# A decoder layer on one core: rotating q and k from the product banks, inverse roots as logarithm, exponential and correction, and the sums of squares as two single-rate products

## The chip, the cores and the metric

One core of a Trainium2 chip runs the whole program. The metric is the device time of one execution in microseconds (us); lower is better. Three executions of the kernel before are given, and one further execution was recorded by the profiler.

## The reference, cut to what matters

One layer with 1024 channels, 2048 prompt columns and 8 sample columns. All arithmetic is float32.

```
h  = RMSNorm(x)*(1+scale1)+shift1          # scale, shift, g from silu(c) @ w_ada
[u | q | k | v | a_pool | a_attn] = h @ w_in
q = rope(rmsnorm_per_head(q) * q_norm_g)   # 12 heads of 64, 3 groups of 4 heads
k = rope(rmsnorm_per_head(k) * k_norm_g)
x += g1 * ( sig(a_pool)*(PoolMix(u) @ w_pool_br) + sig(a_attn)*(DilatedAttn(q,k,v) @ w_attn_br) ) @ w_out
h2 = RMSNorm(x)*(1+scale2)+shift2
x += g2 * relu(h2 @ w_up)^2 @ w_down
```

rmsnorm multiplies by 1/sqrt(mean of squares + 1e-6); rope maps the halves (a, b) of each head to (a cos - b sin, b cos + a sin).

## The kernel before

**Numbers.** A float32 product is made of three products of the rounded type F32R: each operand is split into a high part (a cast) and a low part (the difference), and `mm3` runs high x high, high x low, low x high. The weights are split by ScalarE (`wh`, L183) and GpSimd (`wh`, L184) as their loads arrive; activations are split where they are made. A plain float32 product also exists (`small`, L168), which the kernel uses for sums over channels.

**Stages, in the order of the trace.** Columns go in two halves: ci=0 has 1032 columns (pieces of 512, 256 and 264; the last holds the 8 samples), ci=1 has 1024 (two of 512). The opening (to about 81 us) makes the modulation and the first normed columns. qkv(0) follows (to about 295 us) with six PSUM banks for products; gates, sample attention and the pool branch come to about 745 us; then qkv(1) runs with two banks only, with the prompt's attention between its products (to about 1140 us); more attention and the merger to 1380 us; w_out, the second norm and the MLP to the end at 3060 us.

**One job of q or k** is one group g of four heads (2 x 128 channels: the heads' first halves in i=0, second halves in i=1), q or k, and one piece of columns: 18 jobs in qkv(0) (six of each size), 12 in qkv(1). For each, `dense` fills two banks `ps_qk` of 24 matmuls each. `qk_out` reads each bank twice on ScalarE: L390 copies it with the norm's gain to `ab`, L391 squares it to `qsq`. Then the generator `after_qk` runs: SyncE loads the cosines and sines `cs` (L404, 512 KB), GpSimd adds the two squares (L405) and makes two of the four products of the rotation (L409, L411), VectorE the other two (L410, L412) and the sum and the difference `ro` (L413, L414). At `yield HS_AT` it sleeps for 6500 ns of TensorE's planned time; then TensorE sums squares over each head's channels with the fp32 matmul `ps_hs` against the 0/1 matrix `hones` (L417, which is part of the constants `cp`), ScalarE takes the root (L419), VectorE the reciprocal (L420) and the two products with it (L422). ScalarE and GpSimd split the result into `ohl` (L444, L445), one buffer, which SyncE stores to `qst` or `kst` in HBM (L450 to L456).

**Order.** TensorE's program order is worked out by class `Order`: each matmul adds its planned nanoseconds to `now`, and a generator that yields a number is resumed when `now` has passed it. So the place of `ps_hs` among the dense products is fixed in the program. The other engines' orders are set by the Tile framework's scheduler from the same program, with a higher priority for what stands under `first()`. Each engine works through its own list in order, and an instruction that waits holds all behind it. SyncE issues all loads and stores from one list.

**The norms of x** go through `rms_finish`: a fp32 matmul with `ones` gives the sum of squares, then the same pair of root (L313, ScalarE) and reciprocal (L314, VectorE); ten times in all, two of them (`rs0`, `rs1`) in the opening.

## Time and profile before

| what | value |
|---|---|
| median of 3 runs | 3061.22 us (3057.11 to 3063.97) |
| the profiled execution's own time | 3062.32 us |
| its span, first to last instruction | 3060.5 us |
| TensorE busy | 2933.8 us (96%) |
| ScalarE, GpSimd, VectorE busy | 982.3, 966.2, 1590.5 us |
| mean granted TensorE clock | 0.980 |

TensorE is busy nearly all the time, so a change shows in the time where it shortens TensorE's own work, or where it makes TensorE wait more or less. The share is a mean over stages; the windows in the section of rows keep them apart. A granted clock of 1.00 is TensorE's upper level of 2.4 GHz and 0.50 the lower of 1.2 GHz; a window's value between them is a mean.

### The profile page before, as it was taken

The page shows a single profiled execution, that of the slowest core. Times are in us where ns is not written, and L with a number is a line of the kernel's source. Part 1 is how long each engine was busy: PE and PEld are TensorE (multiplying, and loading weights), DVE is VectorE, ACT ScalarE, POOL GpSimd, SP SyncE. Part 2 cuts the span into 40 slices and gives each one's busy share as a digit, 9 for nine tenths or more (in the row PEclk, how much of TensorE's full clock was granted, in tenths as well). Part 3 has the DMA queues.
Part 4 walks back from the last instruction along what each step waited for, and adds up shares of the span by engine and source line. Part 5 has one row for each costly group of instructions (what it writes and reads, how often), then busy time and mean ns, then how long its engine had stood idle before and what let it go on. Part 6 is the DMA issues. An engine that isn't in the chain of part 4 may idle for free.

```text
span 3060.5 us, 40917 instructions
## 1 busy us (share of the span) xinstructions
PE 2933.8 (96%) x16220; PEld 2510.3 (82%) x16220; DVE 1590.5 (52%) x2649; ACT 982.3 (32%) x1772; POOL 966.2 (32%) x510
## 2 busy tenths in 40 slices
PE   6899999999898799999999999999999999999999
PEld 3899788887787688878899999999877888888887
DVE  5556442541744534456865545555677554444444
ACT  5333342433554534433521221121235211111211
POOL 2665341433533312233532122122245312221221
PEclk7999999999999889999999999999999999999999
DMA  6544752335777779876321111111272211111111
GB/s 239 172 144 154 270 183 92 118 118 151 200 196 203 186 191 229 239 243 218 105 78 48 43 49 49 42 51 47 92 242 83 76 42 56 48 49 42 55 43 69
DMA packets 207599, 379.09 MB, mean 124 GB/s; under 512 B 47424, under 2 KB 103072, under 8 KB 206624
## 3 DMA queue, kind: packets, MB, share of 16 engines
q1 hardware_dynamic: 195888, 359.63, 38.6%
q10 hardware_dynamic: 11520, 16.85, 1.5%
q8 instruction: 128, 2.10, 0.3%
q14 instruction: 63, 0.52, 0.1%
HBM read 294.89 MB, written 81.75 MB: 123 GB/s over the span
## 4 chain that ended last, share of the span: by engine, by line
PE 76%; DMA 5%; DVE 5%; issue 4%; POOL 3%; ACT 2%; SPq 1%; ACTq 0%; DVEq 0%; POOLq 0%
PE ps_dn L153 23%; PE ps_up L153 22%; PE ps_g L153 10%; PE ps_v L153 4%; PE ps_qk L153 4%; PE ps_wo L153 3%; PE ps_u L153 3%; PE ps_o L153 1%; PE ps_pb L153 1%; POOL wh L184 1%; PE ps_s L153 1%; PE ps_ada L153 1%; DMA slab<-kst 1%; DMA cs<-in_rope 1%; PE ps_ab L153 1%
## 5 line engine op out<-in xcount | busy, mean ns | idle before, releaser
L184 POOL TENSOR_TENSOR wh<-wr,wh 128x1024 fp32r<-128x1024 f32 (+1 forms) x274 | 649.3, 2377 | 1637.9 <-ACT wh L183 1620.7
L153 PE MATMUL ps_dn<-rt,wh 128*128 128x512 f32 (+2 forms) x3840 | 727.0, 350 | 5.3 <-POOL wh L184 3.3
L153 PEld LDWEIGHTS ps_dn<-rt,wh 128*128 128x128 f32 x3840 | 619.6, 188 | 108.2 <-POOL wh L184 4.2
L183 ACT CAST wh<-wr 128x1024 fp32r<-128x1024 f32 (+1 forms) x306 | 309.4, 1023 | 737.9 <-issue 564.0
L1306 DVE SCALAR_TENSOR_TENSOR xa<-ps_dn,mod,xa 128x512 f32<-128x512 f32 (+1 forms) x640 | 405.2, 642 | 202.1 <-PE ps_dn L153 195.9
L153 PE MATMUL ps_g<-h,wh 128*128 128x512 f32 (+2 forms) x1920 | 389.6, 354 | 0.4 <-POOL wh L184 0.4
L153 PE MATMUL ps_up<-hb,wh 128*128 128x264 f32 (+2 forms) x2304 | 371.7, 319 | 0.0
L153 PE MATMUL ps_up<-ha,wh 128*128 128x512 f32 x1536 | 367.3, 395 | 0.0
L153 PEld LDWEIGHTS ps_up<-hb,wh 128*128 128x128 f32 x2304 | 332.3, 188 | 36.1
L153 PEld LDWEIGHTS ps_g<-h,wh 128*128 128x128 f32 x1920 | 307.2, 190 | 48.5 <-POOL wh L184 1.0
L153 PEld LDWEIGHTS ps_up<-ha,wh 128*128 128x128 f32 x1536 | 286.6, 188 | 66.3 <-issue 0.5
L153 PE MATMUL ps_qk<-h,wh 128*128 128x512 f32 (+2 forms) x1440 | 301.4, 362 | 14.2 <-POOL wh L184 4.9
L1290 DVE TENSOR_TENSOR r<-r 128x512 f32<-128x512 f32 (+2 forms) x160 | 99.3, 621 | 389.2 <-ACT r L1289 389.1
L153 PEld LDWEIGHTS ps_qk<-h,wh 128*128 128x128 f32 x1440 | 233.6, 193 | 58.5 <-POOL h L327 6.3
L1292 DVE TENSOR_TENSOR rt<-r,rt 128x512 fp32r<-128x512 f32 (+2 forms) x160 | 218.0, 1362 | 81.7 <-ACT rt L1291 81.6
L1289 ACT ACTIVATE r<-ps_up 128x512 f32<-128x512 f32 (+2 forms) x160 | 82.1, 513 | 416.8 <-PE ps_up L153 416.8
L153 PE MATMUL ps_v<-wh,h 128*128 128x256 f32 (+1 forms) x1224 | 171.6, 297 | 25.4 <-ACT wh L183 19.3
L153 PEld LDWEIGHTS ps_v<-wh,h 128*128 128x128 f32 (+1 forms) x1224 | 157.8, 195 | 30.5 <-ACT wh L183 19.7
L945 ACT ACTIVATE pe<-pe,ost 128x128 f32<-128x128 f32 (+1 forms) x192 | 87.1, 454 | 142.5 <-DVE ost L943 139.5
L943 DVE CUSTOM_DVE_ANT_0 pe<-ps_s,cp 128x128 f32<-128x128 f32 (+1 forms) x192 | 61.5, 358 | 118.2 <-PE ps_s L153 118.0
L1291 ACT CAST rt<-r 128x512 fp32r<-128x512 f32 (+2 forms) x160 | 85.7, 536 | 66.4 <-DVE r L1290 66.4
L445 POOL TENSOR_TENSOR ohl<-ro,ohl 128x256 fp32r<-128x256 f32 (+1 forms) x66 | 76.1, 1175 | 92.4 <-ACT ohl L444 81.8
(182 smaller groups left out, 2981.7 us busy)
## 6 DMA issues: line engine op xcount, KB each, us to landing
wr<-in_w_up SPq DMA_DIRECT2D x72, 512.0 KB
wr<-in_w_down SPq DMA_DIRECT2D x68, 512.0 KB
wr<-in_w_in SPq DMA_DIRECT2D x64, 512.0 KB
wr<-in_w_ada SPq DMA_DIRECT2D x48, 512.0 KB
slab<-kst SPq DMA_DIRECT2D x40, 512.0 KB
wr<-in_w_out SPq DMA_DIRECT2D x32, 512.0 KB
cs<-in_rope SPq DMA_DIRECT2D x18, 512.0 KB
qst<-ohl SPq DMA_DIRECT2D x9, 1024.0 KB
```

Of the source, the lines that this page charges most:

```text
L153: PE.matmul(ps, w, x, start=start, stop=stop)
L183: S.copy(out=wt[:, 0, :n], in_=raw[:, :n])
L184: eng.tensor_tensor(out=wt[:, 1, :n], in0=raw[:, :n], in1=wt[:, 0, :n].bitcast(F32), op=ALU.subtract)
L445: G.tensor_tensor(out=pl, in0=pi, in1=ph.bitcast(F32), op=ALU.subtract)
L943: V.tensor_tensor_reduce(out=pe[:, off:off + nk], in0=ps[:, off:off + nk], in1=mask[:, mo:mo + nk], scale=-0.125, scalar=3.0e38, op0=ALU.a ...
L945: S.activation(out=pe[:, off:off + nk], in_=pe[:, off:off + nk], func=AF.Exp, scale=-1.0, bias=o[:, 64:65], accum_out=o[:, 65:66])
L1289: S.activation(out=r1[:, :l], in_=ps[:, :l], func=AF.Relu)
L1290: V.tensor_tensor(out=r1[:, :l], in0=r1[:, :l], in1=r1[:, :l], op=ALU.mult)
L1291: S.copy(out=rt[:, 0, a:a + l], in_=r1[:, :l])
L1292: V.tensor_tensor(out=rt[:, 1, a:a + l], in0=r1[:, :l], in1=rt[:, 0, a:a + l].bitcast(F32), op=ALU.subtract)
L1306: V.scalar_tensor_tensor(out=x[:, c0 + a:c0 + a + lp], in0=ps[:, :lp], scalar=mod[:, 40 + m, 0:1], in1=x[:, c0 + a:c0 + a + lp], op0=ALU.m ...
```

## The change

1. `qk_out` becomes `Job.out`. VectorE makes all four products of the rotation straight from the banks (L423: bank x gain x cosine or sine, two instructions for each bank); ScalarE keeps only the square (L425). The copies to `ab` and GpSimd's two products go. The load of `cs` is issued before the job's dense products, with two buffers in both halves (before: one in qkv(1)); `rt` has two buffers.
2. Root and reciprocal become `inv_root`: on ScalarE a logarithm (L311) and an exponential (L312), on VectorE a correction of three instructions (L313 to L315). Factors of the correction are folded into the products that use it.
3. The sum of squares over a head is two F32R products: ScalarE casts the squares (`sqhl`, L437), VectorE takes the difference (L438). The tiles for these have the tag `th` with two buffers: a job of 512 columns takes both, a smaller one takes one. `hones` becomes an F32R tile of its own, which the opening loads and casts.
4. HS_AT goes from 6500 to 9000.

```diff
-HS_AT = 6500
+HS_AT = 9000
...
-    def rms_finish(np_, psp, acc, splits):
+    def inv_root(out, x, n, w):
+
+        S.activation(out=out, in_=x, func=AF.Ln, scale=1.0 / n, bias=epsc)
+        S.activation(out=out, in_=out, func=AF.Exp, scale=-0.5)
+        V.scalar_tensor_tensor(out=w, in0=x, scalar=n * EPS, in1=out, op0=ALU.add, op1=ALU.mult)
+        V.tensor_tensor(out=w, in0=w, in1=out, op=ALU.mult)
+        V.scalar_tensor_tensor(out=out, in0=w, scalar=-3.0 * n, in1=out, op0=ALU.add, op1=ALU.mult)
+
+    def rms_finish(np_, psp, acc, splits, w):
         rs = np_.tile([P, 520], F32, tag="rs", bufs=1, name="rs")
         for c0, n in splits:
             ps = psp.tile([P, 512], F32, tag="st", name="ps_st")
             small(ps[:, :n], ones, acc[:, c0:c0 + n], n / 0.6)
-            S.activation(out=rs[:, c0:c0 + n], in_=ps[:, :n], func=AF.Sqrt, scale=1.0 / D, bias=epsc)
-            V.reciprocal(out=rs[:, c0:c0 + n], in_=rs[:, c0:c0 + n])
+            inv_root(rs[:, c0:c0 + n], ps[:, :n], D, w[:, c0:c0 + n])
         return rs
 
     def modulated(hf, x, xr, rs, n, i, k, dst, c0, samp, eng):
 
         sh = (0 if i == 0 else 24) + k
-        V.tensor_tensor(out=xr, in0=x, in1=rs[:, :n], op=ALU.mult)
+        V.scalar_tensor_tensor(out=xr, in0=x, scalar=-0.5 / D, in1=rs[:, :n], op0=ALU.mult, op1=ALU.mult)
...
-    def qk_out(qk, i, ab, sq, ps, n):
-        with first():
-            S.activation(out=ab[:, i, :n], in_=ps[:, :n], func=AF.Copy, scale=qkg[:, qk, i:i + 1])
-            S.activation(out=sq[:, i, :n], in_=ps[:, :n], func=AF.Square)
...
-        def after_qk(g, qk, t0, n, ab, sq):
+        class Job:
+
+
+            def __init__(self, g, qk, t0, n):
+                self.g, self.qk, self.t0, self.n = g, qk, t0, n
+                c = BASE[ci] - 1024 * ci + t0
+                self.cs = ap.tile([P, 2, 512], F32, tag="cs", bufs=2, name="cs")
+                SP.dma_start(out=self.cs[:, :, :n], in_=I["rope"][:, :, c:c + n])
+                self.sq = ap.tile([P, 2, 512], F32, tag="qsq", bufs=2, name="qsq")
+                self.o = ap.tile([P, 2, 512], F32, tag="ro", bufs=2, name="ro")
+                self.t = ap.tile([P, 2, 512], F32, tag="rt", bufs=2, name="rt")
+
+            def out(self, i, ps):
+                n = self.n
+                with first():
+                    for j, dst in ((i, self.o[:, i, :n]), (1 - i, self.t[:, 1 - i, :n])):
+
+                        V.scalar_tensor_tensor(out=dst, in0=ps[:, :n], scalar=qkg[:, self.qk, i:i + 1],
+                                               in1=self.cs[:, 0 if j == i else 1, :n], op0=ALU.mult, op1=ALU.mult)
+                    S.activation(out=self.sq[:, i, :n], in_=ps[:, :n], func=AF.Square)
+
+        def after_qk(job):
+            g, qk, t0, n, sq, o, t = job.g, job.qk, job.t0, job.n, job.sq, job.o, job.t
             samp = ci == 0 and t0 + n == 1032
             npr = n - NS if samp else n
-            cs = ap.tile([P, 2, 512], F32, tag="cs", bufs=2 - ci, name="cs")
-            SP.dma_start(out=cs[:, :, :n], in_=I["rope"][:, :, BASE[ci] - 1024 * ci + t0:BASE[ci] - 1024 * ci + t0 + n])
             G.tensor_tensor(out=sq[:, 0, :n], in0=sq[:, 0, :n], in1=sq[:, 1, :n], op=ALU.add)
-            a, b, co, si = ab[:, 0, :n], ab[:, 1, :n], cs[:, 0, :n], cs[:, 1, :n]
-            t = ap.tile([P, 2, 512], F32, tag="rt", bufs=1, name="rt")
-            o = ap.tile([P, 2, 512], F32, tag="ro", bufs=2, name="ro")
-            G.tensor_tensor(out=t[:, 0, :n], in0=b, in1=si, op=ALU.mult)
-            V.tensor_tensor(out=o[:, 0, :n], in0=a, in1=co, op=ALU.mult)
-            G.tensor_tensor(out=t[:, 1, :n], in0=a, in1=si, op=ALU.mult)
-            V.tensor_tensor(out=o[:, 1, :n], in0=b, in1=co, op=ALU.mult)
+
+            m = 1 if n > 256 else 2
+            hl = [gtp.tile([P, m, 512 // m], F32R, tag="th", bufs=2, name="sqhl") for _ in range(2 // m)]
+            sh, sl = (hl[0][:, 0, :n], hl[-1][:, m - 1, :n])
+            with first():
+                S.copy(out=sh, in_=sq[:, 0, :n])
+                V.tensor_tensor(out=sl, in0=sq[:, 0, :n], in1=sh.bitcast(F32), op=ALU.subtract)
             V.tensor_tensor(out=o[:, 0, :n], in0=o[:, 0, :n], in1=t[:, 0, :n], op=ALU.subtract)
             V.tensor_tensor(out=o[:, 1, :n], in0=o[:, 1, :n], in1=t[:, 1, :n], op=ALU.add)
             yield HS_AT
             pst = stp.tile([P, 512], F32, tag="st", name="ps_hs")
-            small(pst[:, :n], hones, sq[:, 0, :n], n / 0.6)
+            mm(pst[:, :n], hones, sh, True, False, max(107.0, n / 2.4 + 2.5))
+            mm(pst[:, :n], hones, sl, False, True, max(107.0, n / 2.4 + 2.5))
             rs = ap.tile([P, 512], F32, tag="qrs", bufs=2 - ci, name="qrs")
-            S.activation(out=rs[:, :n], in_=pst[:, :n], func=AF.Sqrt, scale=1.0 / 64, bias=epsc)
-            V.reciprocal(out=rs[:, :n], in_=rs[:, :n])
+            inv_root(rs[:, :n], pst[:, :n], 64, t[:, 0, :n])
             for i in range(2):
-                V.tensor_tensor(out=o[:, i, :n], in0=o[:, i, :n], in1=rs[:, :n], op=ALU.mult)
+                V.scalar_tensor_tensor(out=o[:, i, :n], in0=o[:, i, :n], scalar=-1.0 / 128, in1=rs[:, :n], op0=ALU.mult, op1=ALU.mult)
...
                 for c0, n in subs(ci)[1 if ws else 0:]:
-                    ab = ap.tile([P, 2, 512], F32, tag="ab", bufs=2, name="ab")
-                    sq = ap.tile([P, 2, 512], F32, tag="qsq", bufs=2, name="qsq")
+                    job = Job(g, qk, ci * 1024 + c0, n)
                     for i in range(2):
                         ps = mmp.tile([P, 512], F32, tag="mm", name="ps_qk")
                         dense(ps, wts[i], hb, c0, n)
-                        qk_out(qk, i, ab, sq, ps, n)
-                    last[0] = od.spawn(after_qk(g, qk, ci * 1024 + c0, n, ab, sq))
+                        job.out(i, ps)
+                    last[0] = od.spawn(after_qk(job))
             wv = [weights("w_v", g, kk) for kk in range(2)]
             tiles = [(j * P, P) for j in range(8)] + ([] if ci else [(1024, NS)])
...
+        raw = rawp.tile([P, 1024], F32, tag="wr", name="wr")
+        SP.dma_start(out=raw[:, :P], in_=I["hones"])
+        S.copy(out=hones, in_=raw[:, :P])
```

In the built program the number of table loads on ScalarE goes from 32 to 77: each logarithm and each exponential of an `inv_root` has a load ahead of it.

ScalarE's list in qkv(0), the six jobs of group 1, of the kernel before. 128x512, 128x256 and 128x264 are the three pieces of q, then of k.

```order
76 L390 ACTIVATE ab<-ps_qk,cp 128x512
77 L391 ACTIVATE qsq<-ps_qk 128x512
...
84 L419 ACTIVATE qrs<-ps_hs,epsc 128x512
85 L390 ACTIVATE ab<-ps_qk,cp 128x264
86 L391 ACTIVATE qsq<-ps_qk 128x264
87 L183 CAST wh<-wr 128x1024
88 L390 ACTIVATE ab<-ps_qk,cp 128x264
89 L391 ACTIVATE qsq<-ps_qk 128x264
90 L183 CAST wh<-wr 128x1024
91 L444 CAST ohl<-ro 128x512 x2
92 L419 ACTIVATE qrs<-ps_hs,epsc 128x256
```

The squares of the third piece (86, 89) stand ahead of the first piece's split (91), with one root between them and the second piece. The same jobs in the changed kernel:

```order
95 L437 CAST sqhl<-qsq 128x256
96 L311 ACT_TABLE_LOAD
97 L311 ACTIVATE qrs<-ps_hs,epsc 128x512
98 L312 ACT_TABLE_LOAD
99 L312 ACTIVATE qrs<-qrs 128x512
100 L183 CAST wh<-wr 128x1024
101 L470 CAST ohl<-ro 128x512 x2
102 L311 ACT_TABLE_LOAD
103 L311 ACTIVATE qrs<-ps_hs,epsc 128x256
104 L312 ACT_TABLE_LOAD
105 L312 ACTIVATE qrs<-qrs 128x256
106 L425 ACTIVATE qsq<-ps_qk 128x264 x2
```

The squares of the third piece (106) have moved behind the first piece's split (101, L470 is the former L444) and the second piece's logarithm and exponential, and the cast for its sum of squares (107, not shown) stands behind them. Further down the same list, for k of the same group:

```order
116 L183 CAST wh<-wr 128x1024
117 L311 ACT_TABLE_LOAD
118 L311 ACTIVATE qrs<-ps_hs,epsc 128x512
119 L312 ACT_TABLE_LOAD
120 L312 ACTIVATE qrs<-qrs 128x512
121 L183 CAST wh<-wr 128x1024
122 L470 CAST ohl<-ro 128x512
123 L425 ACTIVATE qsq<-ps_qk 128x256 x2
124 L437 CAST sqhl<-qsq 128x256
125 L470 CAST ohl<-ro 128x512
```

Here the second piece's squares (123) stand behind half of the first piece's split (122); before, they stood ahead of the root of the first piece.

SyncE's list in qkv(1) about the load of the last v weights (`in_w_v`), of the kernel before and then of the changed one. L989 and L1016 are the same store of attention results, L456 and L482 the same store of keys.

```order
330 L989 DMA att_79<-ost 128x4x66 x4
331 L981 DMA vt<-vscr 128x8x256
332 L404 DMA cs<-in_rope 128x2x512
333 L456 DMA kst_74<-ohl 512x1x512
334 L180 DMA wr<-in_w_v 128x1024
335 L180 DMA wr<-in_w_in 128x1024 x4
```

```order
331 L413 DMA cs<-in_rope 128x2x512
332 L1016 DMA att_79<-ost 128x4x66 x2
333 L482 DMA kst_74<-ohl 512x1x512
334 L1016 DMA att_79<-ost 128x4x66
335 L1008 DMA vt<-vscr 128x8x256
336 L180 DMA wr<-in_w_v 128x1024
337 L180 DMA wr<-in_w_in 128x1024 x4
```

The load of `cs` has moved up; the weights' load still stands behind the store of the keys.

## Rows read from the trace of the kernel before

**Rows 1.** Windows by stage: length, each engine's busy us, clock, DMA share, GB/s.

```profile
110.00:295.00 185.00, 181.89 (x1288) 167.51 (x1287) 102.59 (x146) 64.78 (x119) 111.93 (x94) 0.99 0.52 163
...
745.00:1000.00 255.00, 232.17 (x1355) 201.69 (x1353) 133.84 (x250) 128.40 (x266) 106.14 (x62) 0.95 0.77 200
1000.00:1140.00 140.00, 112.54 (x640) 103.15 (x640) 52.33 (x162) 57.88 (x167) 34.81 (x21) 0.89 0.78 185
```

**Rows 2.** Waits in 110 to 295 us: total, times, longest.

```profile
ACT ohl L444 <- DMA qst<-ohl: 29.3, 7, 5.8
ACT ohl L444 <- DMA kst<-ohl: 27.1, 5, 8.5
...
PE ps_hs L153 <- POOL qsq L405: 3.0, 2, 2.5
```

**Rows 3.** Waits in 745 to 1000 us, columns as in rows 2.

```profile
POOL rt L411 <- DMA cs<-in_rope: 23.4, 4, 12.0
...
PE ps_o L153 <- DVE ost L963: 6.4, 6, 1.5
PE ps_o L153 <- ACT px L953: 5.5, 2, 3.5
```

**Rows 4.** Waits in 1000 to 1140 us.

```profile
PE ps_v L153 <- ACT wh L183: 16.2, 1, 16.2
```

**Rows 5.** Chain of waits, 871 to 874 us: start, duration, what.

```profile
871.54 0.91 PE ps_hs L153 x2
872.46 1.39 PE ps_qk L153 x6
```

**Rows 6.** Groups by line: count | busy us, mean ns | idle before, releasers.

```profile
L1306 DVE SCALAR_TENSOR_TENSOR xa<-ps_dn,mod,xa 128x512 f32<-128x512 f32 (+1 forms) x640 | 405.2, 642 | 202.1 <-PE ps_dn L153 195.9
...
L390 ACT ACTIVATE ab<-ps_qk,cp 128x512 f32<-128x512 f32 (+2 forms) x60 | 36.1, 602 | 95.0 <-PE ps_qk L153 83.8 <-DVE ro L412 7.5 <-POOL wh L184 3.5
...
L153 PE MATMUL ps_hs<-qsq,cp 128*128 128x512 f32 (+2 forms) x60 | 26.2, 519 | 5.1 <-POOL qsq L405 5.1
...
L419 ACT ACTIVATE qrs<-ps_hs,epsc 128x512 f32<-128x512 f32 (+2 forms) x30 | 18.2, 606 | 9.9 <-PE ps_hs L153 9.7
L419 ACT ACT_TABLE_LOAD x12 | 15.4, 1283 | 0.2
```

**Rows 7.** VectorE from 764 us, in order of time: start, duration, line.

```profile
764.63 0.69 DVE L410 TENSOR_TENSOR ro<-ab,cs 128x512 f32<-128x512 f32 x1 [5.14 <-DMA cs<-in_rope]
765.24 1.78 DVE L412 TENSOR_TENSOR ro<-ab,cs 128x512 f32<-128x512 f32 x1
...
772.05 3.34 DVE L420 RECIPROCAL qrs<-qrs 128x512 f32<-128x512 f32 x1
```

**Rows 8.** Groups by line in 110 to 295 us.

```profile
L444 ACT CAST ohl<-ro 128x256 fp32r<-128x256 f32 (+1 forms) x36 | 20.8, 615 | 68.7 <-DMA qst<-ohl 29.3 <-DMA kst<-ohl 27.1 <-DVE vt L510 7.0
...
L183 ACT CAST wh<-wr 128x1024 fp32r<-128x1024 f32 x17 | 17.7, 1050 | 6.9 <-PE ps_v L153 5.8 <-DMA out_v<-vt 1.1
```

**Rows 9.** Windows about two waits of TensorE, columns as in rows 1.

```profile
120.00:125.00 5.00, 4.49 (x23) 4.43 (x24) 1.78 (x4) 1.09 (x3) 1.87 (x3) 0.66 0.97 322
...
770.00:774.00 4.00, 0.49 (x3) 0.48 (x3) 4.00 (x8) 1.73 (x7) 2.20 (x2) 0.92 0.91 239
774.00:778.00 4.00, 4.00 (x17) 3.16 (x17) 4.00 (x14) 2.31 (x7) 1.13 (x2) 0.50 0.72 169
778.00:782.00 4.00, 4.00 (x18) 3.46 (x19) 1.81 (x4) 3.44 (x10) 3.74 (x4) 0.73 0.24 86
```

**Rows 10.** ScalarE from 764 us, in order of time.

```profile
764.22 1.28 ACT L419 ACT_TABLE_LOAD   x1
765.52 0.69 ACT L419 ACTIVATE qrs<-ps_hs,epsc 128x512 f32<-128x512 f32 x1
```

**Rows 11.** SyncE's issue and ScalarE's cast of the last v weights, in time.

```profile
1061.12 0.62 SPq L180 DMA_DIRECT2D wr<-in_w_v  x1
...
1067.72 1.04 ACT L183 CAST wh<-wr 128x1024 fp32r<-128x1024 f32 x1 [9.25 <-DMA wr<-in_w_v]
```

More of the change, by code (lines that the diff above doesn't have):

```diff
@@ L52 @@
 PRIO = 400
-CPACK = (("cT", (8, 9)), ("bada", (48,)), ("gn", (2, 8)), ("ident", (128,)), ("ones", (128,)), ("hones", (128,)),
+CPACK = (("cT", (8, 9)), ("bada", (48,)), ("gn", (2, 8)), ("ident", (128,)), ("ones", (128,)),
          ("mask", (256,)), ("qkg", (2, 2)), ("psc", (4,)), ("icnt", (4, 16)), ("stT", (4, 8, 15)), ("fold", (9,)),
@@ L237, in emit @@
         off += n
-    cT, ident, ones, hones, mask = cv["cT"], cv["ident"], cv["ones"], cv["hones"], cv["mask"]
+    cT, ident, ones, mask = cv["cT"], cv["ident"], cv["ones"], cv["mask"]
     bada, gn, qkg, icnt, stT = cv["bada"], cv["gn"], cv["qkg"], cv["icnt"], cv["stT"]
+    hones = cst.tile([P, P], F32R, name="hones")
     epsc = cst.tile([P, 1], F32, name="epsc")
@@ L347, in load_x, with sq_tile @@
         return [xt[:, k, :n] for k in range(KD)]
+    def sq_tile():
+        return npl.tile([P, 520], F32, tag="sq", bufs=3, name="rw")
     def x_sum(ci, hi, xs, eng):
@@ L477, in qkv @@
                 for qk in range(2):
-                    ab = ap.tile([P, 2, 512], F32, tag="ab", bufs=2, name="ab")
-                    sq = ap.tile([P, 2, 512], F32, tag="qsq", bufs=2, name="qsq")
+                    job = Job(2, qk, 0, 512)
                     for i in range(2):
@@ L482, in qkv @@
                         mm3(pss[t], wk(ws[t], KD)[4:], hx(hb, KD, 0, 512)[4:], True, start=False)
-                        qk_out(qk, i, ab, sq, pss[t], 512)
-                    last[0] = od.spawn(after_qk(2, qk, 0, 512, ab, sq))
+                        job.out(i, pss[t])
+                    last[0] = od.spawn(after_qk(job))
             for qk in range(2):
@@ L487, in qkv @@
                 for c0, n in subs(ci)[1 if ws else 0:]:
-                    ab = ap.tile([P, 2, 512], F32, tag="ab", bufs=2, name="ab")
-                    sq = ap.tile([P, 2, 512], F32, tag="qsq", bufs=2, name="qsq")
+                    job = Job(g, qk, ci * 1024 + c0, n)
                     for i in range(2):
@@ L492, in qkv @@
                         dense(ps, wts[i], hb, c0, n)
-                        qk_out(qk, i, ab, sq, ps, n)
-                    last[0] = od.spawn(after_qk(g, qk, ci * 1024 + c0, n, ab, sq))
+                        job.out(i, ps)
+                    last[0] = od.spawn(after_qk(job))
             wv = [weights("w_v", g, kk) for kk in range(2)]
@@ L770, in opening @@
         acc = x_sum(0, 0, x0, V)
-        rs0 = rms_finish(npl, stp, acc, HALVES[0][0][2])
+        rs0 = rms_finish(npl, stp, acc, HALVES[0][0][2], sq_tile())
         m0()
@@ L781, in opening @@
         m3 = ada_rows(op, 3, raws[3], sil)
-        rs1 = rms_finish(op, stp, acc, HALVES[0][1][2])
+        rs1 = rms_finish(op, stp, acc, HALVES[0][1][2], sq_tile())
         part(2)
@@ L822, in next_h @@
         yield 20000
-        rs = rms_finish(npl, stp, acc, HALVES[1][0][2])
+        rs = rms_finish(npl, stp, acc, HALVES[1][0][2], sq_tile())
         while not free[0]:
@@ L830, in next_h @@
         yield X2_AT
-        rs = rms_finish(npl, stp, acc, HALVES[1][1][2])
+        rs = rms_finish(npl, stp, acc, HALVES[1][1][2], sq_tile())
         make_h(1, 1, xt, rs, h1[0])
@@ L1248, in norm2 @@
         yield 2500
-        rs = rms_finish(tp, stp, acc, splits)
+        rs = rms_finish(tp, stp, acc, splits, wtile("rw"))
         for k in range(KD):
```

## The prediction

> **What bounds the kernel now.** I read the windows by stage first, because a mean over the program hides where TensorE waits [rows 1]. In qkv(0) TensorE is busy 181.89 of 185 us at a clock of 0.99: only 3.1 us of waiting can be won there, and every new wait costs in full. In the two windows of qkv(1) it is busy 232.17 of 255 and 112.54 of 140 us: 22.8 + 27.5 = 50.3 us of waiting, and the clock is 0.95 and 0.89. So the change can gain mainly in qkv(1) and lose mainly in qkv(0).
>
> The second view is the waits of those stages. In qkv(0) TensorE waits 3.0 us for the operand of `ps_hs`. ScalarE waits far longer there, 29.3 + 27.1 us, for stores of `ohl` to land [rows 2], and yet TensorE is hardly held, since the squares it needs stand ahead of those splits in ScalarE's list. What stands behind what in that list is thus the question. In qkv(1) one wait is large, 16.2 us for the cast of the last v weights; the rest is attention's steps, 6.4 and 5.5 us, and GpSimd waits 23.4 us for `cs` [rows 3, 4].
>
> The third views are groups and single stretches, for prices.
>
> **TensorE's own work.** A fp32 `ps_hs` of 512 columns takes 0.91 us on the chain; six `ps_qk` of 512 take 1.39 us, 0.23 each [rows 5]. Two F32R products cost 0.46 us, so a job of 512 saves 0.45 us, and I take half, 0.22, for 256 and 264 columns (estimate by columns). qkv(0): 6 x 0.45 + 12 x 0.22 = 5.3 us. qkv(1): 12 x 0.45 = 5.4 us. This lies on the path wherever TensorE doesn't wait: sum **-10.7 us**. It is the surest term.
>
> **Prices on the other engines.** The copy L390 took 0.602 us as a mean and goes (two per job). The root took 0.606 us as a mean [rows 6], the reciprocal 3.34 for 512 columns [rows 7]. In their place ScalarE has two loads of 1.283 us [rows 6] and two activations; the trace has no logarithm or exponential of this form, and I take the root's price for each. Bounds: the root's 0.61 (nothing in the rows says less for the same columns) and the root plus another load, 1.9 us. VectorE gets three instructions for the reciprocal; L1306, a product of the same shape with a bank as operand, takes 0.642 us [rows 6], so about 2 us against 3.34. The four L423 likewise take 4 x 0.64 = 2.6 us. Two of the products they replace took 0.69 and 1.78 us in one job [rows 7]; VectorE's load rises little, if at all.
>
> ScalarE, per job: -2 x 0.60 + 2 x 1.28 + 0.61 + a cast of about 0.6 = +2.6 us. In six jobs of a group of qkv(0) that is 15 us more, and ScalarE was busy 64.78 of 185 us [rows 1]: it has room as a sum. Its order is another matter.
>
> **qkv(0), where I expect the loss.** Take group 1 and count from the start of its first dense product. TensorE's list fixes the times: 48 products of 512 end at 48 x 0.23 = 11; the pieces of 256 and 264 take about half of that each and end near 17 and 23; the sums of squares stand at about 21, 26.5 and 33 (9 planned microseconds behind each piece, rounded to the next boundary).
>
> ScalarE's changed list: the second piece's cast of squares (95) must wait until `ps_hs` of the first has freed both `th` tiles, 21.6. Then load, logarithm, load, exponential: 22.1 + 1.28 + 0.69 + 1.28 + 0.69 = 26.0. A weights cast of 1.05 [rows 8]: 27.1. The split of the first piece (101) needs VectorE's three corrections and its product, about 2.7 us behind the exponential, so 28.8, and takes two times 0.62 [rows 8]: 30.1. Load, logarithm, load, exponential of 256 columns: 33.5. Only then the third piece's squares, whose banks were full at 23: 34.2; GpSimd's addition of about 0.7, the cast, VectorE's difference: about 36.5 against 33. TensorE waits **3.5 us**. For k the second piece's squares stand behind half of the split of the first (122), which itself waits for its correction and for the previous store of `ohl`, up to 8.5 us late [rows 2]; I get 4 to 5 us. ScalarE's list has the same order in group 0, so 2 x 8 us, and in group 2, whose first jobs come from the opening, I count about 10: **+26 us**, eight waits. If the stores land early and scheduling slack is greater than I count, perhaps 10; if each split waits for its store as it did [rows 2], 40.
>
> Each such wait costs the clock too: after TensorE had stood still for 3.51 us at 770 to 774, the granted clock was 0.50 and 0.73 in the next two stretches of 4 us, and after 2.5 us it was 0.66 in a stretch of 5 [rows 9]: 3.1 us and 1.5 us lost. Eight waits by 1.5: **+12 us**. Against this, the old waits for that operand go, 5.1 us in all (3.0 in this stage, the rest just ahead of it [rows 2, 6]), with some 3 us of their clock: **-8 us**. With -5.3 of TensorE's work qkv(0) comes to 26 + 12 - 8 - 5 = **+25 us** (+5 to +45).
>
> A rule stands against a part of this. Behind a load at 764.22 us the next activation started at 765.52, so a load cost 1.30 us all in [rows 10]. The Trainium skill's page "ScalarE: Activation LUTs", section "What ACT_TABLE_LOAD costs", puts a drain of about 1.38 us on top of every load, 2.66 in all; by that each wait above, with four loads ahead of it, would be 5.5 us longer, and eight of them 44 us. The measurement decides, and I leave this out. The same page's section "Table sets: the hidden batching unit" says that one set holds both functions, so that a logarithm and the exponential behind it need one load. The built program doesn't use it: it has two loads for each.
>
> **qkv(1), where I expect a gain.** TensorE's list is 5.4 us shorter. `cs` has two buffers and is asked for ahead of the products, so GpSimd's and VectorE's waits for it go (23.4 and, in one place, 5.14 us [rows 3, 7]); GpSimd's two products go; the reciprocal, which held attention's masks behind it for 3.34 us [rows 7], becomes three instructions of 0.64, between which masks can pass. Of 6.4 + 5.5 us [rows 3] I take half, 6, back. Against it: two banks only, and each is now released by VectorE after 1.3 us and by ScalarE's square. The 16.2 us: the weights' load was issued at 1061.12 us and cast at 1067.72 [rows 11]. In the changed list it still stands behind the store of the keys; `cs` no longer stands ahead of that store, and the sum of squares comes 18 products into the next piece. I count 11 to 14 us instead of 16.2, so 4. Sum -5.4 - 6 - 4 = **-15 us** (-30 to +5; ScalarE had two loads per root and mask there already, so loads add nothing).
>
> **The rest.** In the opening the second norm's roots now put two loads and an exponential, about 3.5 us, ahead of two weights casts for which TensorE waits: **+3 us** (0 to 4). In the norms of phase 3 the path from sum to root is 0.69 + 1.28 + 0.69 + 2.0 = 4.6 us against 0.69 + 3.34 = 4.0, with the first load hidden while ScalarE waits for the sum; TensorE works on other products meanwhile, so nothing. If that cover were gone, ten times 0.6 = 6 us. The gates keep their `th` tiles: nothing.
>
> Sum: 3 + 25 - 15 = +13 on the profiled 3062.3, which is 1.1 above the median: **3074 us**.
>
> **Rivals.** (1) *The waits of qkv(0) stay hidden.* The third piece's operand is then ready before 33, as when the split doesn't hold the list, or the loads are overlapped with the activations ahead of them. Then qkv(0) gives -13 (5.3 of work, 8 of waits and clock) and with -15 and +3 the time is 3062.3 - 25 = 3037, 3036 by the median. For it: ScalarE's list was blocked for 56 us without harm [rows 2]; against it: the squares stood ahead then. It decides when the delay of the third piece is under 3 us. Chance 0.28. (2) *Half of the waits*, +13 in qkv(0), cancels with qkv(1): within 6 us of 3061, which is the 0.2% that a measurement of this kernel can tell from no change. Chance 0.13. (3) *VectorE holds the banks in qkv(1).* A bank is free only after two L423, which stand behind masks, corrections and splits in one list; if the dense products wait 1.5 us at half of 24 banks, the gain of 15 becomes a loss of 3: 3062 + 3 + 25 + 3 = 3093, and with the upper bound of qkv(0) 3113. Chance 0.12. The forecast, 3067 to 3090, has 0.47.
>
> **How the numbers follow.** The range goes from inside rival 1 to inside rival 3, 3040 to 3100; what lies outside is 0.2. Faster by over 0.2% is rival 1, 0.28; the same 0.13; slower is the forecast and rival 3, 0.59.
>
> **What would show it.** In the changed profile: `ps_hs` pairs of 0.46 us on the chain; waits of TensorE for `ps_hs` in 110 to 295 us, now on VectorE's difference L438, eight of 3 to 5 us, each with a clock under 0.8 behind it; loads of 1.28 us on L311 and L312, 38 and 37 of them; qkv(1) over its 395 us shorter by some 15, without waits for `cs`. I am wrong if TensorE's idle time in qkv(0) stays at 3 us (rival 1), or if `ps_qk` or `ps_v` waits for L423 in qkv(1) (rival 3).

## The result and the profile after

The changed kernel took 3132.94 us as a median of four runs (3128.23 to 3134.05), the kernel before 3060.4 in runs beside it. The ratio is 1.0234 (95% interval 1.0216 to 1.0252): **slower by 72 us**, where I had forecast 13 us slower and a range up to 3100. The direction was right; the size was off by a factor of more than five.

The profiled execution took 3128.2 us. To find the place I read in the timelines when TensorE begins and ends each stage. A stage is counted here from the first `ps_qk` of a half to its last `ps_v`, and from there on to the first `ps_wo`. Lengths are in us, each from one profiled execution. All kernels of the experiments stand here too, and "hs wait" is TensorE's waiting ahead of `ps_hs` in qkv(0). The ratio is that to runs of the kernel before beside it, whose medians lie between 3060.2 and 3063.5 us, so differences of some 4 us between two kernels say nothing.

| kernel | median | ratio, 95% interval | qkv(0) | qkv(1) | to `ps_wo` | hs wait |
|---|---|---|---|---|---|---|
| before | 3060.4 | | 256.3 | 379.3 | 255.8 | 5.1 |
| changed | 3132.9 | 1.0234, 1.0216 to 1.0252 | 307.8 | 383.8 | 264.6 | 42.6 |
| e1 part 1 alone | 3091.2 | 1.0092, 1.0069 to 1.0114 | 300.1 | 366.4 | 256.5 | 35.4 |
| e2 part 2 alone | 3119.9 | 1.0191, 1.0165 to 1.0217 | 288.5 | 394.5 | 259.1 | 21.1 |
| e3 parts 3, 4 alone | 3087.6 | 1.0085, 1.0065 to 1.0105 | 263.5 | 390.8 | 264.4 | 3.2 |
| e4 without part 2 | 3094.2 | 1.0108, 1.0085 to 1.0130 | 285.6 | 372.9 | 264.9 | 29.0 |
| e5 part 1, square first | 3037.5 | 0.9930, 0.9915 to 0.9945 | 251.0 | 360.0 | 256.6 | 1.0 |
| e6 changed, square first | 3122.7 | 1.0206, 1.0191 to 1.0222 | 289.8 | 393.9 | 265.1 | 6.9 |
| e7 part 4 alone | 3062.6 | 1.0010, 1.0001 to 1.0020 | 256.8 | 362.2 | 271.5 | 0.0 |
| e8 changed, HS_AT 16000 | 3108.4 | 1.0160, 1.0145 to 1.0175 | 300.2 | 360.6 | 267.4 | 24.3 |
| e9 changed, one load | 3088.4 | 1.0092, 1.0076 to 1.0108 | 289.9 | 363.3 | 264.8 | 32.8 |
| e10 e9, square first | 3067.0 | 1.0017, 1.0006 to 1.0027 | 265.2 | 364.5 | 268.0 | 0.0 |
| e11 e4, square first | 3065.6 | 1.0020, 1.0010 to 1.0029 | 259.1 | 373.5 | 263.6 | 0.0 |
| e12 e5, HS_AT 9000 | 3042.7 | 0.9940, 0.9925 to 0.9955 | 256.7 | 350.8 | 264.4 | 0.0 |
| e13 e11, HS_AT 9500 | 3066.4 | 1.0008, 0.9993 to 1.0022 | 256.7 | 368.0 | 276.0 | 0.0 |
| e14 e11, cast on GpSimd | 3087.6 | 1.0089, 1.0069 to 1.0108 | 261.1 | 391.5 | 268.1 | 0.2 |
| e15 e13 and e14 | 3091.1 | 1.0093, 1.0070 to 1.0116 | 267.7 | 377.1 | 275.6 | 2.4 |
| e16 e12, split unused | 3060.2 | 1.0006, 0.9996 to 1.0016 | 265.9 | 368.0 | 264.9 | 0.0 |
| e17 e11, no priority | 3057.8 | 0.9987, 0.9976 to 0.9997 | 251.4 | 373.6 | 265.3 | 2.0 |
| e18 e11, high part twice | 3063.5 | 1.0008, 0.9999 to 1.0018 | 261.8 | 370.2 | 264.8 | 0.0 |

Of the changed kernel's growth qkv(0) has 51.5 us, qkv(1) 4.5 and the attention behind it 8.8. The windows of the changed kernel at its own bounds, columns as in [rows 1]:

```profile
35.00:343.00 308.00, 254.60 (x1598) 227.56 (x1599) 170.77 (x303) 155.72 (x226) 113.33 (x83) 0.88 0.39 124
796.00:1180.00 384.00, 329.89 (x1934) 296.22 (x1933) 177.14 (x466) 186.13 (x431) 99.96 (x58) 0.92 0.73 190
```

and of the kernel before, at its bounds:

```profile
35.00:292.00 257.00, 239.26 (x1599) 213.72 (x1600) 154.65 (x209) 103.58 (x187) 152.09 (x120) 0.96 0.46 148
744.00:1123.00 379.00, 333.37 (x1941) 295.56 (x1939) 185.04 (x406) 185.42 (x431) 136.21 (x81) 0.93 0.77 194
```

In qkv(0) TensorE stands idle for 308.0 - 254.6 = 53.4 us instead of 17.7, and is busy 15.3 us longer though its work is shorter: the clock is 0.88 instead of 0.96. The waits of that stage in the changed kernel, which answer to [rows 2]:

```profile
ACT qsq L425 <- DVE rt L423: 33.9, 17, 6.0
...
PE ps_hs L153 <- ACT sqhl L437: 41.7, 8, 6.9
...
PE ps_qk L153 <- ACT wh L183: 10.0, 2, 5.0
```

Eight waits for `ps_hs`, as forecast, but 41.7 us, and they end with ScalarE's cast L437 and not with the difference L438. The first row was in no step of mine: ScalarE's square of a bank waits for VectorE's two products from the same bank. One of the eight waits, for k of group 1, on TensorE:

```profile
228.49 0.58 PE L153 MATMUL ps_hs<-sqhl,hones 128*128 128x256 f32 x1 [6.94 <-ACT sqhl L437]
```

on ScalarE ahead of it:

```profile
215.50 1.28 ACT L311 ACT_TABLE_LOAD   x1
216.80 0.69 ACT L311 ACTIVATE qrs<-ps_hs,epsc 128x512 f32<-128x512 f32 x1
217.50 1.28 ACT L312 ACT_TABLE_LOAD   x1
218.80 0.63 ACT L312 ACTIVATE qrs<-qrs 128x512 f32<-128x512 f32 x1
219.34 1.04 ACT L183 CAST wh<-wr 128x1024 fp32r<-128x1024 f32 x1
224.44 1.11 ACT L470 CAST ohl<-ro 128x512 fp32r<-128x512 f32 x1 [4.07 <-issue]
225.46 0.89 ACT L425 ACTIVATE qsq<-ps_qk 128x256 f32<-128x256 f32 x2
228.04 0.41 ACT L437 CAST sqhl<-qsq 128x256 fp32r<-128x256 f32 x1 [1.69 <-POOL qsq L431]
```

and on VectorE:

```profile
219.46 0.69 DVE L313 SCALAR_TENSOR_TENSOR rt<-ps_hs,qrs 128x512 f32<-128x512 f32 x1 [6.52 <-ACT qrs L312]
220.19 0.69 DVE L314 TENSOR_TENSOR rt<-rt,qrs 128x512 f32<-128x512 f32 x1
220.91 2.72 DVE L315 SCALAR_TENSOR_TENSOR qrs<-rt,qrs 128x512 f32<-128x512 f32 x1
223.67 0.69 DVE L448 SCALAR_TENSOR_TENSOR ro<-ro,qrs 128x512 f32<-128x512 f32 x1
224.28 0.48 DVE L423 SCALAR_TENSOR_TENSOR ro<-ps_qk,cp,cs 128x256 f32<-128x256 f32 x1
```

GpSimd splits a weight meanwhile:

```profile
220.45 2.64 POOL L184 TENSOR_TENSOR wh<-wr,wh 128x1024 fp32r<-128x1024 f32 x1 [2.48 <-ACT wh L183]
```

The order of the lists locks two engines to each other. ScalarE works on the first piece's root, VectorE waits 6.52 us for it with the second piece's products (224.28) behind the correction, ScalarE's squares of the second piece wait behind the split, and TensorE for them all. The squares themselves hardly wait for the bank here: they start as the split ends. What is late is the split, 5.0 us behind the end of the exponential (219.43 to 224.44). It is the same for q of this group:

```profile
188.07 0.63 ACT L312 ACTIVATE qrs<-qrs 128x512 f32<-128x512 f32 x1
...
193.72 2.13 ACT L470 CAST ohl<-ro 128x512 fp32r<-128x512 f32 x2 [4.08 <-DVE ro L448]
...
199.28 0.80 ACT L425 ACTIVATE qsq<-ps_qk 128x264 f32<-128x264 f32 x2
```

The other kind of wait stands in group 2, which runs first: there the squares come late because VectorE has not yet read the bank.

```profile
140.37 0.49 DVE L423 SCALAR_TENSOR_TENSOR ro<-ps_qk,cp,cs 128x264 f32<-128x264 f32 x1 [2.46 <-DMA out_k<-ro]
141.29 0.39 ACT L425 ACTIVATE qsq<-ps_qk 128x264 f32<-128x264 f32 x1 [2.83 <-DVE rt L423]
```

VectorE itself waits here until a store of keys out of `ro` has landed, and holds the bank with it; before, its products of `ro` read the copies in `ab`.

The clock behind such waits, to be held against [rows 9]:

```profile
228.00:232.00 4.00, 3.31 (x13) 3.01 (x14) 1.90 (x6) 3.44 (x5) 1.56 (x2) 0.50 0.25 89
232.00:236.00 4.00, 4.00 (x28) 4.00 (x28) 3.67 (x9) 2.52 (x5) 0.92 (x1) 0.75 0.78 272
```

In qkv(1) TensorE's waits of [rows 3, 4] are smaller, and new ones stand in their place:

```profile
PE ps_v L153 <- ACT qsq L425: 10.2, 3, 6.9
PE ps_v L153 <- ACT wh L183: 9.6, 2, 6.9
PE ps_qk L153 <- ACT qsq L425: 8.1, 1, 8.1
```

The last is the stage's beginning. SyncE issues `cs` behind the two v weights and eight loads of attention:

```profile
794.43 5.88 SPq L180 DMA_DIRECT2D wr<-in_w_v  x2
...
804.82 0.60 SPq L943 DMA_DIRECT2D slab<-kst  x1
805.46 0.60 SPq L413 DMA_DIRECT2D cs<-in_rope  x1
```

VectorE's first product waits for it, and the only two banks are held until then:

```profile
812.99 0.75 DVE L423 SCALAR_TENSOR_TENSOR ro<-ps_qk,cp,cs 128x512 f32<-128x512 f32 x1 [39.39 <-DMA cs<-in_rope]
```

Two prices were right. One is a `ps_hs` pair:

```profile
936.21 1.45 PE ps_qk L153 x6
937.66 0.49 PE ps_hs L153 x2
```

The other is a load, 1.283 us with the next activation right behind it (215.50 to 216.80 above); 38 of the 40 logarithms and 37 of the 40 exponentials have one:

```profile
L311 ACT ACT_TABLE_LOAD x38 | 48.8, 1283 | 0.7
L312 ACT ACT_TABLE_LOAD x37 | 47.5, 1283 | 0.7
```

### The profile page after: what moved, and what is told of

It reads as the page before. It is cut to its first block, busy times and chain, and to the rows that moved or that the text cites. A ratio compares the mean times of both kernels' runs of the same rounds, so it can differ in the third digit from the quotient of the medians.

```text
span 3126.3 us, 40998 instructions
## 1 busy us (share of the span) xinstructions
PE 2944.5 (94%) x16220; PEld 2524.3 (81%) x16220; DVE 1592.8 (51%) x2819; ACT 1050.5 (34%) x1828; POOL 893.4 (29%) x450
## 4 chain that ended last, share of the span: by engine, by line
PE 57%; DVE 4%; DMA 4%; issue 3%; ACT 2%; POOL 2%; SPq 1%; POOLq 0%; ACTq 0%; DVEq 0%
PE ps_dn L153 22%; PE ps_up L153 22%; PE ps_wo L153 4%; PE ps_g L153 3%; PE ps_qk L153 2%; PE ps_o L153 1%; DMA slab<-kst 1%; PE ps_s L153 1%; POOL wh L184 1%; PE ps_ab L153 1%; PE ps_v L153 1%; PE ps_t L172 1%; POOL ohl L471 1%; DMA wr<-in_w_attn_br 1%; DVE t L1215 0%
## 5 line engine op out<-in xcount | busy, mean ns | idle before, releaser
L153 PE MATMUL ps_qk<-h,wh 128*128 128x512 f32 (+2 forms) x1440 | 310.7, 372 | 27.5 <-ACT wh L183 10.0
L153 PEld LDWEIGHTS ps_qk<-h,wh 128*128 128x128 f32 x1440 | 245.2, 203 | 69.3 <-ACT wh L183 11.3
L153 PE MATMUL ps_v<-wh,h 128*128 128x256 f32 (+1 forms) x1224 | 174.8, 300 | 23.6 <-ACT qsq L425 10.2
```

What stands on the lines that cost most here:

```text
L153: PE.matmul(ps, w, x, start=start, stop=stop)
```

## The experiments

### Each part alone, and the change without part 2

e1 and e2 are the kernel before with part 1 and with part 2 of the diff, e3 with parts 3 and 4, where the split stands behind the rotation's sum and difference in the program; e4 is the changed kernel with

```diff
-        S.activation(out=out, in_=x, func=AF.Ln, scale=1.0 / n, bias=epsc)
-        S.activation(out=out, in_=out, func=AF.Exp, scale=-0.5)
-        V.scalar_tensor_tensor(out=w, in0=x, scalar=n * EPS, in1=out, op0=ALU.add, op1=ALU.mult)
...
+        S.activation(out=out, in_=x, func=AF.Sqrt, scale=1.0 / n, bias=epsc)
+        V.reciprocal(out=out, in_=out)
```

and factors of 1.0 in the two products that use it.

> The kernel before with part 1 alone: rotation from the product banks with cosines and sines loaded early, and two buffers of rt; root and reciprocal, the fp32 sum of squares and HS_AT 6500 stay. The theory of the long root (two table loads and three corrections per job hold ScalarE's and VectorE's lists, and the sum of squares comes late) expects 3045 to 3060 us, and no wait of TensorE for the sum of squares over 2 us in qkv(0). The rival of the shared bank (in the changed kernel ScalarE's square waits 33.9 us in qkv(0) for VectorE's two products from the same bank) expects most of the loss here already: 3080 to 3110.

> The kernel before with part 2 alone: logarithm, exponential and correction in place of root and reciprocal, 77 table loads. The theory of the long root expects the larger part of the loss, 3080 to 3110 us, with table loads ahead of the squares on ScalarE and waits of TensorE for the sum of squares' operand. The rival of the shared bank expects at most 3070, since here ScalarE alone reads the banks.

> The kernel before with part 3 and 4 alone: sum of squares as two single-rate products, cast and difference, HS_AT 9000. Both theories expect a gain of TensorE's own work, 10.7 us, less some waits: 3045 to 3058 us. A third theory, that the th tiles (a 512 piece takes both) hold up the next piece's cast, expects 3065 to 3085 and waits of TensorE on the cast.

> The changed kernel with part 2 undone: root and reciprocal again, 32 table loads, parts 1, 3 and 4 stay. The theory of the long root expects 3050 to 3075 us and the waits for the sum of squares (41.7 us) down to under 10. The rival of the shared bank expects 3100 to 3130, with the waits nearly as before.

Measured: 3091.2, 3119.9, 3087.6 and 3094.2 us. e1 is in the rival's range. e2 is above both of its expectations, e3 above both bands of its own, and e4 lies between its two. Each is slower than the kernel before, e1 to e3 by 26 to 58 us (the ratio's excess of 3060), so no single cause is enough: part 1 loses in qkv(0) (+43.8) and gains in qkv(1) (-12.9); part 2 loses in both (+32.2 and +15.2); parts 3 and 4, from which both theories expected a gain, lose in qkv(0) (+7.2), in qkv(1) (+11.5) and behind it (+8.6). e4 keeps 29.0 of the 42.6 us of waits, so most of them come without the long root; e2 has 21.1, so the long root alone makes such waits too. In e1's qkv(0) the waits, and the row on which the rival rests, are:

```profile
PE ps_hs L153 <- POOL qsq L426: 35.4, 8, 5.9
```

```profile
ACT qsq L420 <- DVE rt L418: 64.4, 29, 6.0
```

### Who reads the bank first, and where the sum of squares stands

e5 is e1, and e6 the changed kernel, with one line moved:

```diff
                 with first():
+                    S.activation(out=self.sq[:, i, :n], in_=ps[:, :n], func=AF.Square)
                     for j, dst in ((i, self.o[:, i, :n]), (1 - i, self.t[:, 1 - i, :n])):
...
-                    S.activation(out=self.sq[:, i, :n], in_=ps[:, :n], func=AF.Square)
```

e7 is the kernel before with `HS_AT = 9000`, e8 the changed kernel with `HS_AT = 16000`.

> As e1 (the kernel before with part 1 alone), but ScalarE's square of a bank is put ahead of VectorE's two products from that bank in the program. Theory of the bank in turns: two engines read a bank one after the other, in the program's order, so in e1 each square waited for VectorE's list (64.4 us in qkv(0)), and TensorE's waits for the sum of squares came from that. It expects the waits for the sum of squares to fall from 35.4 to under 10 us, qkv(0) from 300 to 255 to 270 us long, and the whole at 3045 to 3062 us. The rival, that VectorE's and ScalarE's lists are interleaved wrongly whoever reads first, expects qkv(0) at 285 us or more and 3075 to 3095.

> The changed kernel with ScalarE's square of a bank ahead of VectorE's two products. The theory of the bank in turns expects the waits for the sum of squares to fall from 41.7 us to 10 to 20 (what the long root alone cost in e2), and 3090 to 3115 us. The rival, that the table loads and the splits ahead of the squares in ScalarE's list hold them, expects 3122 to 3135 and 35 us or more of those waits.

> The kernel before with HS_AT 9000 alone. In e3 (parts 3 and 4) qkv(1) was 11.5 us and the attention behind it 8.6 us longer than before. If the later place of the sum of squares in TensorE's list did that, this kernel is at 3070 to 3085 us with both stretches longer; if the two products with their cast and difference did it, it is within 6 us of before.

> The changed kernel with HS_AT 16000: the sum of squares stands 7 planned microseconds later in TensorE's list, more than the longest wait of 6.9 us. If the operand is only late by a fixed amount, the waits for it fall below 10 us, qkv(0) shortens by 35 to 50 us and the time is 3085 to 3100, but for what the later place costs in qkv(1). The rival, that the lists of the engines run after each other (a later sum of squares makes the roots and with them the next squares later too), expects half of the waits or more to stay, and 3110 to 3140.

e5 took **3037.5 us, 0.7% less than the kernel before** and less than its theory expected: one moved line is worth 54 us against e1 (50 by the ratios). The waits for `ps_hs` fell from 35.4 us to this one, and ScalarE's square waits for TensorE alone:

```profile
PE ps_hs L153 <- POOL qsq L426: 1.0, 1, 1.0
```

```profile
ACT qsq L416 <- PE ps_qk L153: 52.3, 25, 4.9
```

The line does two things at once. The square no longer waits until VectorE has read the bank, and in ScalarE's built list the third piece's squares stand ahead of the first piece's split again, as they did in the kernel before. In q of group 1 of e6, to be held against 193.72 and 199.28 above:

```profile
181.53 0.37 ACT L421 ACTIVATE qsq<-ps_qk 128x264 f32<-128x264 f32 x1
...
186.85 2.14 ACT L470 CAST ohl<-ro 128x512 fp32r<-128x512 f32 x2 [3.66 <-DVE ro L448]
```

No run separates the two. With the long root the same line is worth 10 us only (e6, 3122.7, by the rival's expectation in the time; the waits of 6.9 us are below even the theory's): qkv(0) is 18.0 us shorter, qkv(1) 10.1 us longer. The waits for `ps_hs` go in e6 too, but others stand in qkv(0): VectorE, held in its corrections, now frees the banks late.

```profile
PE ps_qk L153 <- ACT wh L183: 10.0, 2, 5.0
PE ps_v L153 <- DVE rt L424: 9.0, 3, 5.0
PE ps_qk L153 <- DVE rt L424: 6.5, 1, 6.5
PE ps_hs L153 <- ACT sqhl L437: 6.0, 2, 3.2
```

e7 is within 0.2% of before: part 4 shortens qkv(1) by 17.1 us and lengthens what follows by 15.7. e8, between its two expectations in time, keeps 24.3 of 42.6 us of waits, as the rival expected, and in qkv(0) TensorE now waits for the squares to free the banks. Of its 24.5 us against the changed kernel, 23.2 are in qkv(1).

```profile
PE ps_qk L153 <- ACT qsq L425: 8.6, 1, 8.6
PE ps_v L153 <- ACT qsq L425: 7.1, 1, 7.1
```

### The loads, and all causes of qkv(0) together

In e9 both activations of `inv_root` use one function, so one load serves the program, with every other instruction kept; e10 is e9 with e5's moved line; e11 is e4 with that line moved, and e12 is e5 with `HS_AT = 9000`.

```diff
-        S.activation(out=out, in_=x, func=AF.Ln, scale=1.0 / n, bias=epsc)
+        S.activation(out=out, in_=x, func=AF.Exp, scale=-1e-9, bias=epsc)
```

> The changed kernel with an exponential in place of the logarithm, so that one set of functions serves all of ScalarE: one table load instead of 77, every other instruction kept (what the roots give is not the reference's then). If the loads are what makes the long root dear, this comes to 3090 to 3105 us, near e4 with root and reciprocal (3094). The rival, that VectorE's three corrections and ScalarE's second activation in the chain do it, expects 3118 to 3130.

> As e9, and with ScalarE's square ahead of VectorE's products as in e6: parts 1 to 4 without their loads and with the bank's other order (the roots' values are not the reference's). If the two causes, bank in turns and loads, are the whole of the loss, it comes to 3030 to 3060 us; if the corrections on VectorE hold the banks' products as well, to 3075 to 3110 with TensorE waiting for VectorE's products L424.

> The changed kernel with part 2 undone as in e4 and the square ahead as in e5: parts 1, 3 and 4. The theory of the bank in turns expects a fall of about 35 to 55 us against e4, as from e1 to e5 (54 us): 3035 to 3058. If part 3's cast and difference cost what e3 showed (24 us against before) whatever the order, it is at 3055 to 3068.

> As e5 (part 1 with the square ahead), with HS_AT 9000 as in the change. In e5 TensorE waits only 1.0 us for the sum of squares in qkv(0), so the theory expects no gain there and the same time within 10 us: 3030 to 3048.

e9: 3088.4, so the 76 loads are worth 44.5 us, a little below the expected band: 17.9 in qkv(0) and 20.5 in qkv(1). This isn't the price of the loads that the change adds, because the kernel before has 32 of its own. In qkv(0) it has none and the changed kernel 38; in qkv(1) both have 24. So the 17.9 us are the change's, while the 20.5 us of qkv(1) come from loads as many as the kernel before has there. e10: 3067.0, between the two bands; without the loads and with the line moved, 65.9 of the 72.5 us are gone, and 42.6 of the 51.5 in qkv(0). e9's 32.8 us of waits are gone too, and 24.9 us of TensorE's idle time in qkv(0) stay (265.2 - 240.3 busy), part of it for VectorE's products, 10.6 us. e11: 3065.6, in its second band, 28.6 us below e4, yet 22.9 above e12 (3042.7, as expected), which differs by part 3 alone. e10 and e11 are 1.4 us apart: part 2 with one load in the program costs as much as root and reciprocal with 32, so its longer chain isn't priced alone by any run.

### Why part 3 costs more than it saves

e13 is e11 with `HS_AT = 9500`; e14 is e11 with the high part written by GpSimd; e15 is both. e14's edit:

```diff
-            G.tensor_tensor(out=sq[:, 0, :n], in0=sq[:, 0, :n], in1=sq[:, 1, :n], op=ALU.add)
...
             with first():
-                S.copy(out=sh, in_=sq[:, 0, :n])
+                G.tensor_tensor(out=sh, in0=sq[:, 0, :n], in1=sq[:, 1, :n], op=ALU.add)
+                G.tensor_tensor(out=sq[:, 0, :n], in0=sq[:, 0, :n], in1=sq[:, 1, :n], op=ALU.add)
```

e16 is e12 with the split made beside the fp32 product:

```diff
             G.tensor_tensor(out=sq[:, 0, :n], in0=sq[:, 0, :n], in1=sq[:, 1, :n], op=ALU.add)
...
+            with first():
+                S.copy(out=sh, in_=sq[:, 0, :n])
+                V.tensor_tensor(out=sl, in0=sq[:, 0, :n], in1=sh.bitcast(F32), op=ALU.subtract)
...
             small(pst[:, :n], hones, sq[:, 0, :n], n / 0.6)
```

e17 is e11 without the `with first()` around the split, e18 is e11 without the difference, the second product taking `sh` again.

> As e11 (parts 1, 3, 4 with root and reciprocal and the square ahead), with HS_AT 9500 instead of 9000. In the built program this puts the load of the last v weights ahead of the store of the keys in SyncE's list, as in e12, where e11 has it behind. If that order is what parts 3 and 4 cost in qkv(1) (e11 373.5 us, e12 350.8), the wait for those weights (10.7 us) goes, qkv(1) falls to 350 to 360 us and the time to 3043 to 3054. If ScalarE's cast and its wait for GpSimd's sum cost it, qkv(1) stays over 365 and the time at 3060 to 3070.

> As e11, with the high part of the sum of squares written by GpSimd (the sum is made twice there, once rounded), so that ScalarE has no cast and no wait for GpSimd's sum; SyncE's list keeps the late load of the v weights. If the order of that load is the cost, the time stays within 6 us of e11 (3065.6); if ScalarE's cast is, it falls to 3040 to 3055.

> e13 and e14 together. If only the load's order matters, as e13 within 6 us; if both do, 3030 to 3042, which would be the first kernel in which part 3's saving of TensorE's work (10.7 us) shows beside e5 (3037).

> As e12 (part 1 with the square ahead, HS_AT 9000, one fp32 product, 3042.7 us), with ScalarE's cast and VectorE's difference of part 3 made as well and read by nobody. If these two, ahead of attention's steps in their lists, are what part 3 costs, the time rises by 15 to 35 us, to 3058 to 3078; if TensorE's two products or their place cost it, it stays within 8 us of e12.

> As e11 (3065.6 us), with the cast and the difference without their higher priority. If the cost is that they stand ahead of attention's steps, it falls to 3040 to 3056; if it is their work or th, it stays at 3060 to 3072.

> As e11, without VectorE's difference: the high part is multiplied twice (the sums of squares are not the reference's then), and one th tile is taken per job. If VectorE's difference and the second th tile are the cost, the time falls to 3040 to 3056; if ScalarE's cast behind GpSimd's sum is, it stays at 3058 to 3070.

The load's order is not it, by e13's second expectation: in e13 that wait falls from 10.7 to 0.5 us and qkv(1) is 5.5 us shorter, but what follows is 12.4 longer. e14 and e15, outside both of their expectations, were 22 and 25 us slower than e11 and e13: GpSimd's second sum costs more than dropping ScalarE's cast gives, so they don't clear the cast either. e16 is the clear one, in its first band: cast and difference, read by nobody, cost 17.5 us (3060.2 against 3042.7); in its profiled execution, which is 7 us above its median, qkv(1) is 17.2 us longer than in e12 and qkv(0) 9.2. e17 took 3057.8, 8 us below e11 and between the two expectations, so the priority is a part of it. e18 (3063.5) is 2 us below e11, so the difference and the second `th` tile cost little, and by its second expectation the cast is what is left.

## Why the prediction was wrong

**Right:** the direction, the stage that loses most, the eight waits for `ps_hs`, the clock behind each (0.50 to 0.68 in the 4 us from each late `ps_hs`), loads of 1.28 us without more behind them, 0.46 us for a pair (0.49), a loss of a few us on the weights casts of the opening (`ps_qk` waits 10.0 us for them instead of 3.9, forecast +3), nothing in phase 3 (1677.4 us from the first `ps_wo` to the last `ps_dn` before, 1678.1 after).

The kernels above make a path from the kernel before to the changed one, with one edit at a step. Differences are in us, by stage as in the table of the result:

| step | edit | time | qkv(0) | qkv(1) | to `ps_wo` |
|---|---|---|---|---|---|
| before to e5 | part 1 with the square first | -22.9 | -5.3 | -19.3 | +0.8 |
| e5 to e12 | part 4 | +5.2 | +5.7 | -9.2 | +7.8 |
| e12 to e11 | part 3 | +22.9 | +2.4 | +22.7 | -0.8 |
| e11 to e6 | part 2 | +57.1 | +30.7 | +20.4 | +1.5 |
| e6 to changed | the square behind VectorE's products | +10.2 | +18.0 | -10.1 | -0.5 |
| sum | | +72.5 | +51.5 | +4.5 | +8.8 |

The prices depend on the path: the square's place is worth 10 us here and 54 from e1 to e5, and part 2 is 38.7 from e4 to the changed kernel. On either path part 2 is the largest loss of the changed kernel.

**The steps that failed** are three terms of the sum: the waits of qkv(0) with their clock (26 + 12), part 3 (-10.7), and part 2 in qkv(1), which had no cost.

**qkv(0), forecast +25, measured +51.5.** The mechanism was right, and the waits were mis-sized: 41.7 us in eight instead of 26. Four of them are those of groups 1 and 0, 23.3 us instead of 16. There the squares follow within 0.4 us when ScalarE comes to them, as I had counted. The split ahead of them was late: I had it 2.7 us behind the exponential, and it came 5.0 us behind in all four, since the correction's last instruction L315 took 2.72 to 2.78 us beside GpSimd's split of weights, where I had 0.64. The other four, in group 2, took 18.5 us instead of about 10. There the step "Only then the third piece's squares, whose banks were full at 23: 34.2" fails: the squares also wait until VectorE has read the bank (2.83 us at 141.29), and I had priced VectorE's four products as load alone. That step is worth 18.0 us of qkv(0) in the changed kernel (e6), together with the place in ScalarE's list that comes with it. The Trainium skill's page "PSUM — Partial Sum Buffer", section "PSUM bank collisions raise a hardware error", says that two different engines must not be on the same 32-partition quadrant of a bank at once, two reads included, so the program has to put them in turns; the rows show the turns (33.9 and 64.4 us of ScalarE waiting), no run here shows a collision.

The clock was forecast as 12 us, 1.5 for each wait, and is about 20: busy time rose 15.3 us while the work fell by 5.3 (estimate of the forecast). My own row for a wait of 3.51 us gave 3.1; I had taken the price of a wait of 2.5 for waits of 3.5 to 5.

**qkv(1), forecast -15, measured +4.5.** Part 1 gives its gain (-19.3 with the square first), and so does part 4 (-9.2). Parts 3 and 2 take back 22.7 and 20.4. "Loads add nothing" is right as a count, 24 before and after, but part 2 makes this stage 10.9 (from e4), 15.2 (from before to e2) or 20.4 us longer, where I had expected that masks could pass between its short instructions. VectorE waits 46.6 us there for the exponential. How much of it is the second load between the sum and the correction stays open, since e9 and e10 also take away the old ones.

Rival 3 came true in its mechanism: TensorE waits 18.3 us there for banks (8.1 and 10.2) against its 18. But e5, with its gain of 19.3, has 10.8 us of such waits too (8.5 and 2.3), so they are only a part of what turned the gain into a loss. The sentence "`cs` is asked for ahead of the products" looked at the program and not at SyncE's list, where `cs` stands behind attention's loads: VectorE still waits 43.5 us for it, 39.4 of them up to the stage's first product.

**Part 3**, "the surest term", -10.7 us: TensorE's own time for `ps_hs` did fall, from 25.8 us (e12) to 16.6 (e11), and only to 21.6 in the changed kernel, where the clock is lower. But the whole part costs 22.9 us, 17.5 of them by cast and difference alone (e16). I had given the cast 0.6 us of ScalarE's time per job, had put cast and difference on the path to `ps_hs` in qkv(0), and had given them no place on a path in qkv(1). What makes up the rest, and which share of the 17.5 is ScalarE's waiting for GpSimd's sum (9.8 us in e16's qkv(1)), stays open.

**Part 2's loads** were priced right one by one, and the chain of four of them was the right one. The Trainium skill's page "ScalarE: Activation LUTs", section "Table sets: the hidden batching unit", says that one set has both functions; no run here builds that, but e9, with one load in the whole program, bounds what it would give, 44.5 us.

**Behind qkv(1)** the forecast had no term. The +8.8 us come with HS_AT: every kernel with 9000 or more has 7.8 to 20.2 there (e7 with nothing else has 15.7), e1, e2 and e5 with 6500 have 0.7 to 3.3.

Early loading of `cs` with the old rotation wasn't tried, nor was one set for both functions.

## What to carry to other kernels

When a second engine is to read a product bank, look in the built order which of the two reads first, and let the one whose result TensorE needs next be first: here that was worth 54 us with the short root and 10 with the long one. An instruction moved to an engine inherits everything ahead of it in that engine's list, so a term like "-10.7 us of TensorE's work" is safe only when the operand's new steps are put on a path too. A function whose table must be loaded again for every call is paid in the lists of all engines that wait for its result. And to learn what each part of a change costs, build the path from one kernel to the other an edit at a time, and read it by stage: a stage whose sum is small, as qkv(1) here, can hide gains and losses of 20 us.
